# S5 outputs: the copies of the scan states dealt anew to GpSimd, ScalarE and VectorE, and the gated unit's first weights asked for ahead of y

## The chip, the cores and the metric

One core of a Trainium2 chip runs the whole program. The metric is the device time in microseconds (us), smaller is better. The engines are TensorE (PE in the profile, its weight loads PEld), VectorE (DVE), ScalarE (ACT), GpSimd (POOL) and SyncE (SP), whose queue issues most of the DMAs.

## The reference, cut to what matters

The program is a trunk of two layers over 512 latent and 256 context tokens of width 1024, all in fp32. Each layer is a half-step SwiGLU network, a token mixer and another half-step SwiGLU network. The mixer of layer 0 is a bidirectional S5 state space model, that of layer 1 gated linear attention (GLA). The change lies at the end of the S5 mixer:

```
y = scan forward(u) + flip(scan backward(flip u)) + d_skip * u      # states times C, both directions
z = gelu(y) @ w_glu + b_glu                                         # 1024 -> 2048
val, gate = split(z, 2);   x = x + gate_mod * (val * sigmoid(gate)) # the gated unit
```

## The kernel before

Products of fp32 matrices are made from three products of parts: `mm3` (L113 to L115) multiplies a weight's high half `whi` with the high and the low part of the activation, and its low half `wlo` with the high part. `whi` is cast by ScalarE (L88), `wlo` is a subtraction on VectorE (L89). Both follow the weight's DMA into `wraw`, which SyncE issues; `wraw` has four buffers, `whi` and `wlo` five each.

The scan runs on VectorE and leaves its states in a tile `r` (`big` in the profile). `outputs` makes the result in eight tiles, kt = 0 to 7. For each, `states` copies the states into `xs[kt % 2]`, one of two buffers: per half of the groups (g) and real or imaginary part (a) the forward states (z = 0) in one copy of 64 x 380, the backward states (z = 1) in two, 64 x 124 and 64 x 256. A table of two by two functions, indexed [z][a], names the engine of each copy. For tiles 0 and 1 the first 80 steps are copied early by ScalarE, beside the scan. Then TensorE makes 16 sums of two products (L912), VectorE adds the skip term half by half (L914), ScalarE applies the gelu (L916), and SyncE stores y to DRAM. While tiles 1 to 3 run, the y stored before is read back (`yk`, three buffers); the other five are read back in `glu`.

`glu` first casts each yk into the parts of `h` (two casts on ScalarE, two subtractions on VectorE per k; L937 and L938). `h` lies in the memory of the scan states, so that the first cast waits until all copies of tile 7 are done. Then, for each j, it asks for two weights (q = 0 the value, q = 1 the gate) and `step` multiplies.

The order on each engine is not that of the code: a scheduler simulates the program's timeline when it is built and puts each engine's instructions, and each queue's DMAs, in the order of its plan, for the whole program.

Of the kernel before, what the change touches and what calls it, by code (L numbers as in the profile page):

```python
# [15 lines left out]
P = 128  # L16
D = 1024
# [10 lines left out]
def fview(t, off, dims, p0=0, n=P):  # L28

    b = t[p0:p0 + n]  # L30
    return bass.AP(b.tensor, b.offset + off, [list(b.ap[0])] + [list(d) for d in dims])


def dview(ap, off, dims):

    return bass.AP(ap.tensor, ap.offset + off, [list(d) for d in dims])
# [286 lines left out]
def kinds(s, e):  # L323

    return [(i, max(s, a), min(e, z)) for i, (a, z) in enumerate(((0, CTX), (CTX, TOK))) if max(s, a) < min(e, z)]
# [146 lines left out]
N5 = TOK // L5  # L472
# [4 lines left out]
class S5:  # L477
# [323 lines left out]
    def states(self, kt, kind, evac):  # L801


        c, nc, r = self.c, self.c.nc, self.r
        n0, n = ((0, NX5), (NX5, N5 - NX5))[kind]
        m = (32, 64)[kind]
        u = self.u[kt][:, :, n0:n0 + n]
        banks = [c.bank() for _ in range(kind + 1)]
        for part in range(2):
            for z in range(2):  # L810
                i = (part * 2 + z) * 4 * n
                b, o = banks[i // 512], i % 512
                for q in range(4):
                    for g in range(2):
                        for p0 in range(64 * g, 64 * g + 64, m):
                            nc.tensor.matmul(b[p0:p0 + m, o + q * n:o + (q + 1) * n],
                                             self.rm[2 * kt + part][:, z * 512 + q * P + p0:z * 512 + q * P + p0 + m],
                                             u[:, 2 * q + g], start=True, stop=True)
                src = fview(b, o + z * (n - 1), [(n, 4), (1 - 2 * z, n)])
                dst = fview(r, n0 * P + part * 64 + z * 32 + 4 * kt, [(1, 4), (P, n)])  # L820
                last = (nc.scalar.copy if evac[part] else nc.vector.tensor_copy)(out=dst, in_=src)
        return last
# [38 lines left out]
    def outputs(self, pool, ahead, yp, last):  # L861


        c, nc, r = self.c, self.c.nc, self.r
        loaded, self.ys = {}, []

        def load(kt):
            om = [c.spare() for _ in range(2)]
            for z in range(2):
                c.dma(om[z], self.O[kt][z])  # L870
            return om
        for kt in range(ahead):
            loaded[kt] = load(kt)
        xs = [pool.tile([P, 2, 8, N5], F32, name=f"xs{i}", tag=f"xs{i}", bufs=1) for i in range(2)]
        for x in xs:
            nc.gpsimd.memset(x[:, 0, :, 0:1], 0.0)
        def states(kt, s0, s1, copies):

            x = xs[kt % 2]
            nc.gpsimd.memset(x[:, 1, :, NX5 - 1:NX5], 0.0)  # L880
            for g in range(2):
                for a in range(2):
                    def move(z, lo, hi, to, step):

                        lo, hi = max(lo, s0), min(hi, s1)
                        if lo >= hi:
                            return
                        at, to = (lo, to(lo)) if step > 0 else (hi - 1, to(hi - 1))
                        src = fview(r, at * P + a * 64 + z * 32 + 4 * kt, [(1, 4), (step * P, hi - lo)], 64 * g, 64)
                        dst = fview(x, z * 8 * N5 + g * N5 + to, [(2 * N5, 4), (1, hi - lo)], 64 * a, 64)  # L890
                        copies[z][a](out=dst, in_=src)
                    move(0, 0, N5 - 1, lambda s: s + 1, 1)
                    move(1, 0, NX5 - 1, lambda s: NX5 - 2 - s, -1)
                    move(1, NX5 - 1, N5 - 1, lambda s: NX5 + N5 - 2 - s, -1)
        early = 80
        with c.tc.issue_after(last.ins):
            for kt in range(2):
                states(kt, 0, early, [[nc.scalar.copy] * 2] * 2)

        def work():  # L900
            for kt in range(KT):
                x = xs[kt % 2]
                om = loaded.pop(kt) if kt in loaded else load(kt)
                states(kt, early if kt < 2 else 0, N5, [[nc.scalar.copy, nc.gpsimd.tensor_copy], [nc.vector.tensor_copy] * 2])
                y = pool.tile([P, 8, N5], F32, tag="y5", name="y5", bufs=4)
                for h in range(2):
                    b = c.bank()
                    for i in range(4):
                        g = 4 * h + i
                        o = b[:, i * N5:(i + 1) * N5]  # L910
                        for z in range(2):
                            nc.tensor.matmul(o, om[z][:, g * P:(g + 1) * P], x[:, z, g], start=(z == 0), stop=(z == 1))  # L912
                    yh = y[:, 4 * h:4 * h + 4].rearrange("p g n -> p (g n)")
                    nc.vector.tensor_tensor(out=yh, in0=b[:, :4 * N5], op=ALU.add,  # L914
                                            in1=self.u[kt][:, 4 * h:4 * h + 4].rearrange("p g n -> p (g n)"))
                nc.scalar.activation(y, y, AF.Gelu_apprx_tanh)  # L916
                c.dma(dview(self.Y, kt * P * TOK, [(N5, P), (C5 * TOK, 8), (1, N5)]), y)
                if 0 < kt < 4:
                    self.load_y(yp, kt - 1)
        return work  # L920

    def glu(self, pool, parts, last, after):


        c, nc, m = self.c, self.c.nc, self.m
        wg = self.ins["s5_w_glu"][0].rearrange("(k p) e -> p k e", p=P)
        yh, yl = c.h[:, 0], c.h[:, 1]
        for k in range(KT):
            if k >= len(self.ys):
                self.load_y(pool, k)  # L930
            y = self.ys[k]
            for lo, hi, view in ((0, CTX, lambda t: t.rearrange("p (n i) -> p i n", i=L5)),
                                 (CTX, TOK, lambda t: t.rearrange("p (w i r) -> p i r w", i=L5, r=8))):
                h, l, src = view(yh[:, k, lo:hi]), view(yl[:, k, lo:hi]), y[:, :, lo // L5:hi // L5]
                if lo:
                    src = src.rearrange("p i (r w) -> p i r w", r=8)
                nc.scalar.copy(out=h, in_=src)  # L937
                nc.vector.tensor_tensor(out=l, in0=src, in1=h.bitcast(F32), op=ALU.subtract)  # L938

        def step(j, w, s, e):  # L940
            n = e - s
            banks = [c.bank() for _ in range(2)]
            order = [(k, q) for k in range(KT) for q in range(2)] if j == 0 else \
                    [(k, q) for q in range(2) for k in range(KT)]
            for i, (k, q) in enumerate(order):
                c.mm3(banks[q][:, :n], w[q], slice(k * P, (k + 1) * P), (yh[:, k, s:e], yl[:, k, s:e]),
                      k == 0, k == KT - 1)
                if i % 4 == 3:
                    c.tick()
            sg = c.tmp.tile([P, 512], F32, tag="sg", name="sg", bufs=2)[:, :n]  # L950
            nc.scalar.activation(sg, banks[1][:, :n], AF.Sigmoid, bias=m.col("s5_b_glu", KT + j))
            nc.vector.scalar_tensor_tensor(out=sg, in0=banks[0][:, :n], scalar=m.col("s5_b_glu", j), in1=sg,
                                           op0=ALU.add, op1=ALU.mult)
            for i, a, z in kinds(s, e):
                nc.vector.scalar_tensor_tensor(out=c.xT[:, j, a:z], in0=sg[:, a - s:z - s],
                                               scalar=m.mod[0][:, i, 5, j:j + 1], in1=c.xT[:, j, a:z],
                                               op0=ALU.mult, op1=ALU.add)
        ws = []
        for j in range(KT):
            ws.append([c.weight(wg[:, :, q * D + j * P:q * D + (j + 1) * P]) for q in range(2)])  # L960
            if j < KT - 3:
                for s, e in parts:
                    step(j, ws[j], s, e)
        for s, e in last:
            for j in range(KT - 3, KT):
                step(j, ws[j], s, e)
            after(s, e)
# [645 lines left out]
```

## Time and profile before

| | |
|---|---|
| median of three runs | 2886.12 us (2885.47 to 2887.6) |
| the profiled execution | 2881.74 us, its span 2880.0 us |
| granted TensorE clock, mean | 0.968 of full speed |
| TensorE busy | 2733.7 us, 95% of the span |
| VectorE, ScalarE, GpSimd busy | 1795.0 us (62%), 855.2 us (30%), 22.2 us (1%) |
| the scan's end on VectorE, the outputs' start on TensorE | 801.4 us |
| end of the last output tile on TensorE | 839.7 us |

Times within the program are us from the start of the span. Busy time is the time in which an engine executes; the wait ahead of an instruction is put down to the work that released it last. The profiled execution is a run of its own, so its time lies beside the median and not in it.

### The profile page before, as it was taken

To read this page: it belongs to the slowest core of one execution; us is meant where nothing else is said; L and a number is where in the kernel's file an instruction comes from. 1 tells how busy PE (TensorE), PEld (TensorE's weight loads), DVE (VectorE), ACT (ScalarE), POOL (GpSimd) and SP (SyncE) were. 2 spreads that over 40 slices of the span, in tenths; PEclk is the share of its full clock that TensorE was granted. 3 is DMA by queue.
4 is the path that set the end of the run, shared out by engine and by line. 5 is a ranking of instruction groups with operands and counts; after the bars stand their busy time and mean duration, and the time that the engine had idled before them with its cause. 6 is when DMAs were issued, how large, how long until landed. Compare 5 with 4: busy or idle time off the path is not lost. (4 is left out here: it accounts for less than half of the span.)

```text
span 2880.0 us, 44946 instructions
## 1 busy us (share of the span) xinstructions
PE 2733.7 (95%) x18231; PEld 2577.7 (90%) x18231; DVE 1795.0 (62%) x4080; ACT 855.2 (30%) x1386; POOL 22.2 (1%) x57
## 2 busy tenths in 40 slices
PE   7999999997479999999999999999999899799998
PEld 5899999996269999999999999999998788788887
DVE  6698999436993565556526555665368786643433
ACT  4222222225362422111124221121245453332223
POOL 0000000000010000000000000000000000000000
PEclk9999999997689999999999999999999899899999
DMA  6535554516662133333311342333103112233320
GB/s 226 169 113 158 150 157 137 175 62 193 227 180 81 48 103 109 99 101 116 96 59 38 110 125 88 110 104 95 54 16 89 45 52 67 66 117 95 92 91 30
DMA packets 396045, 305.43 MB, mean 106 GB/s; under 512 B 57995, under 2 KB 344189, under 8 KB 395837
## 3 DMA queue, kind: packets, MB, share of 16 engines
q1 hardware_dynamic: 391228, 293.12, 34.0%
q10 hardware_dynamic: 4608, 9.44, 0.9%
q8 instruction: 143, 2.34, 0.3%
q14 instruction: 66, 0.53, 0.1%
HBM read 275.77 MB, written 30.41 MB: 106 GB/s over the span
## 5 line engine op out<-in xcount | busy, mean ns | idle before, releaser
L115 PE MATMUL bank<-h,wlo 128*128 128x384 f32 (+3 forms) x3160 | 1048.3, 332 | 5.0 <-DVE wlo L89 5.0
L114 PE MATMUL bank<-h,whi 128*128 128x384 f32 (+3 forms) x3160 | 1049.8, 333 | 0.3 <-DVE h L219 0.3
L113 PE MATMUL bank<-h,whi 128*128 128x384 f32 (+3 forms) x3160 | 1044.6, 333 | 2.2 <-ACT h L218 2.2
L88 ACT CAST whi<-wraw 128x1024 fp32r<-128x1024 f32 x313 | 327.5, 1048 | 993.4 <-PE bank L114 934.3
L115 PEld LDWEIGHTS bank<-h,wlo 128*128 128x128 f32 (+1 forms) x3160 | 594.6, 188 | 22.9 <-DVE wlo L89 5.3
L113 PEld LDWEIGHTS bank<-h,whi 128*128 128x128 f32 (+1 forms) x3160 | 593.3, 189 | 22.9 <-ACT h L218 2.7
L114 PEld LDWEIGHTS bank<-h,whi 128*128 128x128 f32 (+1 forms) x3160 | 596.3, 189 | 18.0 <-DVE h L219 0.8
L89 DVE TENSOR_TENSOR wlo<-wraw,whi 128x1024 fp32r<-128x1024 f32 x313 | 381.2, 1219 | 253.0 <-ACT whi L88 245.3
L114 PE MATMUL bank<-ml,whi 128*128 128x384 f32 (+2 forms) x1360 | 447.7, 330 | 0.0
L113 PE MATMUL bank<-mh,whi 128*128 128x384 f32 (+2 forms) x1360 | 446.5, 331 | 0.6 <-DVE xT L279 0.6
L115 PE MATMUL bank<-mh,wlo 128*128 128x384 f32 (+2 forms) x1360 | 446.0, 329 | 0.0
L279 DVE SCALAR_TENSOR_TENSOR xT<-bank,hg,xT 128x256 f32<-128x256 f32 (+2 forms) x488 | 220.7, 499 | 200.2 <-PE bank L115 199.8
L264 DVE TENSOR_TENSOR sg<-sg,bank 128x384 f32<-128x384 f32 (+2 forms) x166 | 89.5, 539 | 355.9 <-PE bank L115 342.7
L113 PEld LDWEIGHTS bank<-mh,whi 128*128 128x128 f32 x1360 | 256.7, 189 | 7.9 <-DVE xT L279 1.0
L114 PEld LDWEIGHTS bank<-ml,whi 128*128 128x128 f32 x1360 | 257.1, 189 | 6.6 <-issue 0.4
L115 PEld LDWEIGHTS bank<-mh,wlo 128*128 128x128 f32 x1360 | 256.2, 188 | 6.5 <-issue 0.2
L427 DVE SCALAR_TENSOR_TENSOR adaacc<-wraw,cs,adaacc 128x512 f32<-128x512 f32 x336 | 236.6, 744 | 14.8 <-DMA wraw<-in_ada_w_dram 14.5
L265 ACT CAST mh<-sg 128x384 fp32r<-128x384 f32 (+2 forms) x166 | 83.4, 502 | 305.9 <-DVE sg L264 304.8
L263 ACT ACTIVATE sg<-bank 128x384 f32<-128x384 f32 (+2 forms) x166 | 79.5, 479 | 199.8 <-PE bank L115 199.8
L266 DVE TENSOR_TENSOR ml<-sg,mh 128x384 fp32r<-128x384 f32 (+2 forms) x166 | 89.8, 541 | 23.5 <-ACT mh L265 23.4
L150 ACT ACTIVATE sq<-xT 128x256 f32<-128x256 f32 (+1 forms) x126 | 52.4, 427 | 59.9 <-DVE xT L279 41.5
L201 DVE SCALAR_TENSOR_TENSOR nt<-xT,sc,bank 128x256 f32<-128x256 f32 (+2 forms) x136 | 61.9, 476 | 12.5 <-PE bank L182 9.3
(298 smaller groups left out, 2332.8 us busy)
## 6 DMA issues: line engine op xcount, KB each, us to landing
wraw<-in_ffn_w_in_dram SPq DMA_DIRECT2D x176, 512.0 KB, 3.8
wraw<-in_ada_w_dram SPq DMA_DIRECT2D x111, 512.0 KB, 3.8
wraw<-in_ffn_w_out_dram SPq DMA_DIRECT2D x88, 512.0 KB, 3.4
wraw<-in_gla_w_in_dram SPq DMA_DIRECT2D x24, 512.0 KB, 3.9
s5R<-s5r ACTq DMA_DIRECT2D x16, 512.0 KB, 3.1
s5O<-s5g SPq DMA_DIRECT2D x64, 128.0 KB, 2.9
wraw<-in_s_w_glu_dram SPq DMA_DIRECT2D x16, 512.0 KB, 4.8
big<-in_ada_w_dram SPq DMA_DIRECT2D x12, 512.0 KB, 8.5
```

The source lines that it names most:

```text
L88: nc.scalar.copy(out=hi[:, :n], in_=raw[:, :n])
L89: nc.vector.tensor_tensor(out=lo[:, :n], in0=raw[:, :n], in1=hi[:, :n].bitcast(F32), op=ALU.subtract)
L113: mm(out, wh, a[0], start=first, stop=False)
L114: mm(out, wh, a[1], start=False, stop=False)
L115: mm(out, wl, a[0], start=False, stop=last)
L201: nc.vector.scalar_tensor_tensor(out=t[:, a - s:z - s], in0=self.xT[:, k, a:z], scalar=sc[i][:, k:k + 1], in1=r[:, a - s:z - s], op0=ALU.m ...
L263: nc.scalar.activation(sg, banks[0][:, :e - s], AF.Silu)
L264: nc.vector.tensor_mul(sg, sg, banks[1][:, :e - s])
L265: nc.scalar.copy(out=mh[:, o], in_=sg)
L266: nc.vector.tensor_tensor(out=ml[:, o], in0=sg, in1=mh[:, o].bitcast(F32), op=ALU.subtract)
L279: nc.vector.scalar_tensor_tensor(out=self.xT[:, d, a:z], in0=banks[d][:, a - s:z - s], scalar=gate[i][:, d:d + 1], in1=self.xT[:, d, a:z], ...
L427: nc.vector.scalar_tensor_tensor(out=acc[:, v], in0=w[:, k], scalar=col, in1=acc[:, v], op0=ALU.mult, op1=ALU.add)
```

## The change

In the table of `outputs` both forward copies go to GpSimd (one was ScalarE's), and of the backward copies those with a = 0 go to ScalarE and those with a = 1 stay on VectorE. The copies of the first 80 steps stay with ScalarE. In `glu`, the call that asks for the weights of j = 0 moves ahead of the loop over y; those of the other j stay where they were. Four lines are added, so that later lines have numbers higher by four (L937 becomes L941, L1243 becomes L1247).

```diff
--- before.py
+++ after.py
@@ -901,7 +901,7 @@
             for kt in range(KT):
                 x = xs[kt % 2]
                 om = loaded.pop(kt) if kt in loaded else load(kt)
-                states(kt, early if kt < 2 else 0, N5, [[nc.scalar.copy, nc.gpsimd.tensor_copy], [nc.vector.tensor_copy] * 2])
+                states(kt, early if kt < 2 else 0, N5, [[nc.gpsimd.tensor_copy] * 2, [nc.scalar.copy, nc.vector.tensor_copy]])
                 y = pool.tile([P, 8, N5], F32, tag="y5", name="y5", bufs=4)
                 for h in range(2):
                     b = c.bank()
@@ -925,6 +925,10 @@
         c, nc, m = self.c, self.c.nc, self.m
         wg = self.ins["s5_w_glu"][0].rearrange("(k p) e -> p k e", p=P)
         yh, yl = c.h[:, 0], c.h[:, 1]
+
+        def weights(j):
+            return [c.weight(wg[:, :, q * D + j * P:q * D + (j + 1) * P]) for q in range(2)]
+        ws = [weights(0)]
         for k in range(KT):
             if k >= len(self.ys):
                 self.load_y(pool, k)
@@ -955,9 +959,9 @@
                 nc.vector.scalar_tensor_tensor(out=c.xT[:, j, a:z], in0=sg[:, a - s:z - s],
                                                scalar=m.mod[0][:, i, 5, j:j + 1], in1=c.xT[:, j, a:z],
                                                op0=ALU.mult, op1=ALU.add)
-        ws = []
         for j in range(KT):
-            ws.append([c.weight(wg[:, :, q * D + j * P:q * D + (j + 1) * P]) for q in range(2)])
+            if j:
+                ws.append(weights(j))
             if j < KT - 3:
                 for s, e in parts:
                     step(j, ws[j], s, e)
```

The names y_8752, y_8784, y_8822, y_8864, y_8906, y_8946, y_8986 and y_9026 below are y of tiles 0 to 7, xs_8663 and xs_8664 the two buffers of the copied states.

SyncE's queue from the store of the first y on; s5Y is y in DRAM, s5O the S5 output matrices. Before:

```order
L70 DMA s5Y<-y_8752 128x8x96
L70 DMA wraw<-s5O_789 128x1024
L70 DMA s5Y<-y_8784 128x8x96
L70 DMA yk<-s5Y 128x768
L70 DMA wraw<-s5O_790 128x1024
L70 DMA s5Y<-y_8822 128x8x96
L70 DMA yk<-s5Y 128x768
L70 DMA wraw<-in_s_w_glu_dram 128x8x128
L70 DMA s5Y<-y_8864 128x8x96
L70 DMA wraw<-in_s_w_glu_dram 128x8x128
L70 DMA yk<-s5Y 128x768
L70 DMA s5Y<-y_8906 128x8x96
```

After the change:

```order
L70 DMA s5Y<-y_8752 128x8x96
L70 DMA wraw<-s5O_789 128x1024
L70 DMA yk<-s5Y 128x768
L70 DMA s5Y<-y_8784 128x8x96
L70 DMA wraw<-s5O_790 128x1024
L70 DMA yk<-s5Y 128x768
L70 DMA s5Y<-y_8822 128x8x96
L70 DMA yk<-s5Y 128x768
L70 DMA wraw<-in_s_w_glu_dram 128x8x128
L70 DMA s5Y<-y_8864 128x8x96
L70 DMA wraw<-in_s_w_glu_dram 128x8x128
L70 DMA s5Y<-y_8906 128x8x96
```

Each of the first three read-backs (yk) stands ahead of the next store of y, and the first weights (in_s_w_glu), which stood behind the second of them, stand behind the third; five more read-backs come later, four of them in a row behind the store of y_8986.

ScalarE around the gelu of tile 4, with the cast of the first weights. Before:

```order
L916 ACTIVATE y_8864<-y_8864 128x768
L891 COPY xs_8663<-big 64x4x95 x2
L916 ACTIVATE y_8906<-y_8906 128x768
L88 CAST whi<-wraw 128x1024
L891 COPY xs_8664<-big 64x4x95 x2
L916 ACTIVATE y_8946<-y_8946 128x768
```

After the change:

```order
L916 ACTIVATE y_8864<-y_8864 128x768
L88 CAST whi<-wraw 128x1024
L891 COPY xs_8663<-big 64x4x31
L891 COPY xs_8663<-big 64x4x64
L891 COPY xs_8663<-big 64x4x31
L891 COPY xs_8663<-big 64x4x64
L916 ACTIVATE y_8906<-y_8906 128x768
```

The cast of the first weights stands ahead of the copies of tile 6 (xs_8663) and of the gelu of tile 4, where it stood behind that gelu; the copies are now the backward shapes.

ScalarE at the end of the outputs, around the gelu of the last tile. Before:

```order
L916 ACTIVATE y_8946<-y_8946 128x768
L937 CAST h<-yk 128x8x32
L937 CAST h<-yk 128x64x8
L937 CAST h<-yk 128x8x32
L937 CAST h<-yk 128x64x8
L937 CAST h<-yk 128x8x32
L937 CAST h<-yk 128x64x8
L916 ACTIVATE y_8986<-y_8986 128x768
L916 ACTIVATE y_9026<-y_9026 128x768
L88 CAST whi<-wraw 128x1024 x2
```

After the change:

```order
L941 CAST h<-yk 128x64x8
L941 CAST h<-yk 128x8x32
L941 CAST h<-yk 128x64x8
L941 CAST h<-yk 128x8x32
L941 CAST h<-yk 128x64x8
L941 CAST h<-yk 128x8x32
L941 CAST h<-yk 128x64x8
L916 ACTIVATE y_9026<-y_9026 128x768
L88 CAST whi<-wraw 128x1024 x2
```

Ahead of the gelu of y_9026 stand now twelve casts of y, all behind the gelu of y_8986; it was six, ahead of that gelu. Behind it follow two casts of weights as before.

VectorE at the same place, the adds of the last tile. Before:

```order
L938 TENSOR_TENSOR h<-yk,h 128x8x32
L938 TENSOR_TENSOR h<-yk,h 128x64x8
L914 TENSOR_TENSOR y_8986<-bank,u 128x384
L938 TENSOR_TENSOR h<-yk,h 128x8x32
L938 TENSOR_TENSOR h<-yk,h 128x64x8
L938 TENSOR_TENSOR h<-yk,h 128x8x32
L938 TENSOR_TENSOR h<-yk,h 128x64x8
L914 TENSOR_TENSOR y_9026<-bank,u 128x384 x2
L89 TENSOR_TENSOR wlo<-wraw,whi 128x1024 x3
```

After the change:

```order
L942 TENSOR_TENSOR h<-yk,h 128x64x8
L942 TENSOR_TENSOR h<-yk,h 128x8x32
L942 TENSOR_TENSOR h<-yk,h 128x64x8
L914 TENSOR_TENSOR y_9026<-bank,u 128x384
L942 TENSOR_TENSOR h<-yk,h 128x8x32
L942 TENSOR_TENSOR h<-yk,h 128x64x8
L942 TENSOR_TENSOR h<-yk,h 128x8x32
L942 TENSOR_TENSOR h<-yk,h 128x64x8
L914 TENSOR_TENSOR y_9026<-bank,u 128x384
L942 TENSOR_TENSOR h<-yk,h 128x8x32
L942 TENSOR_TENSOR h<-yk,h 128x64x8
L89 TENSOR_TENSOR wlo<-wraw,whi 128x1024 x3
```

The first low halves of weights (L89) stood behind the low parts of three yk and stand now behind those of six; between the two adds of the last tile lie four of these subtractions.

TensorE in the GLA stage (layer 1), one of its heads; `gqc` and `gkc` are scaled queries and keys, lines 1110 to 1112 project values. Before:

```order
L1110 MATMUL bank<-whi,h 128x256
L1111 MATMUL bank<-wlo,h 128x256
L1112 MATMUL bank<-whi,h 128x256
L1243 MATMUL aux<-gqc,gkc 128x128 x24
L182 MATMUL bank<-ident,rs 128x128 x4
L1110 MATMUL bank<-whi,h 128x256
L1111 MATMUL bank<-wlo,h 128x256
L1112 MATMUL bank<-whi,h 128x256
```

After the change:

```order
L1114 MATMUL bank<-whi,h 128x256
L1115 MATMUL bank<-wlo,h 128x256
L1116 MATMUL bank<-whi,h 128x256
L1247 MATMUL aux<-gqc,gkc 128x128 x28
L1292 MATMUL aux<-ident,gkf 128x128 x4
L182 MATMUL bank<-ident,rs 128x128 x4
L1114 MATMUL bank<-whi,h 128x256
L1115 MATMUL bank<-wlo,h 128x256
L1116 MATMUL bank<-whi,h 128x256
```

The row of products of gqc and gkc has 28 instead of 24, and four transposes (L1292) have moved up behind it.

## Rows read from the trace of the kernel before

**Rows 1.** The page, part 1: busy time, share of the span and instructions of each engine.

```profile
PE 2733.7 (95%) x18231; PEld 2577.7 (90%) x18231; DVE 1795.0 (62%) x4080; ACT 855.2 (30%) x1386; POOL 22.2 (1%) x57
```

**Rows 2.** The waits of TensorE between 800 and 900 us: engine, tile and line that waited, what it waited for; total us, times, longest.

```profile
PE bank L912 <- POOL xs L891: 41.1, 1, 41.1
PE bank L912 <- DVE xs L891: 5.9, 5, 1.2
PE bank L115 <- DVE wlo L89: 5.0, 1, 5.0
```

**Rows 3.** Stretches of the S5 outputs and of the gated unit's start: stretch and its length in us, then busy us and instructions of PE, PEld, DVE, ACT and POOL, the granted TensorE clock, the DMA share and GB/s.

```profile
805.90:839.70 33.80, 27.86 (x238) 26.88 (x238) 31.32 (x64) 20.17 (x25) 13.07 (x18) 1.00 0.60 174
839.80:843.30 3.50, 0.30 (x2) 0.04 (x1) 3.50 (x6) 2.10 (x4) 0.00 (x0) 1.00 0.76 240
843.40:845.10 1.70, 0.00 (x0) 0.00 (x0) 1.67 (x3) 1.13 (x2) 0.00 (x0) 0.50 0.93 216
845.20:850.10 4.90, 4.90 (x16) 4.90 (x17) 4.32 (x5) 4.90 (x7) 0.00 (x0) 0.50 1.05 310
850.30:900.00 49.70, 49.70 (x285) 49.70 (x285) 25.96 (x35) 21.29 (x28) 0.00 (x0) 1.00 0.57 153
```

**Rows 4.** Timeline of TensorE from 836 to 846 us: start, us, engine, line, operation, out<-in, count, and in brackets the idle time before it and its releaser. L912 is the last tile's products, L113 to L115 those of the gated unit.

```profile
836.79 0.46 PE L912 MATMUL bank<-xs,wraw 128*128 128x96 f32 x2
...
839.49 0.42 PE L113 MATMUL bank<-h,whi 128*128 128x384 f32 x1
...
845.12 0.69 PE L115 MATMUL bank<-h,wlo 128*128 128x384 f32 x1 [5.02 <-DVE wlo L89]
```

**Rows 5.** Timeline of ScalarE from 828 to 853 us (L88 casts a weight's high half, L937 casts y).

```profile
831.16 1.03 ACT L88 CAST whi<-wraw 128x1024 fp32r<-128x1024 f32 x1
...
836.90 4.36 ACT L937 CAST h<-yk 128x256 fp32r<-128x256 f32 x6 [0.68 <-DVE xs L891]
...
850.99 1.70 ACT L937 CAST h<-yk 128x256 fp32r<-128x256 f32 x2 [0.36 <-DMA yk<-s5Y]
```

**Rows 6.** Timeline of VectorE from 834 to 846 us (L938 is the low part of y, L914 the add of a tile, L89 a weight's low half).

```profile
838.53 1.08 DVE L938 TENSOR_TENSOR h<-yk,h 128x512 fp32r<-128x512 f32 x1 [0.30 <-ACT h L937]
...
839.97 3.04 DVE L938 TENSOR_TENSOR h<-yk,h 128x256 fp32r<-128x256 f32 x4
842.91 1.02 DVE L914 TENSOR_TENSOR y<-bank,u 128x384 f32<-128x384 f32 x2
843.85 1.22 DVE L89 TENSOR_TENSOR wlo<-wraw,whi 128x1024 fp32r<-128x1024 f32 x1
```

**Rows 7.** Timeline of VectorE over the state copies of one tile.

```profile
815.35 2.57 DVE L891 COPY xs<-big 64x124 f32<-64x124 f32 x4
...
818.42 1.33 DVE L891 COPY xs<-big 64x124 f32<-64x124 f32 x4
```

**Rows 8.** Instructions by line, operation and shape between 800 and 863 us: line engine op out<-in, count | busy us, mean ns of one | idle time before them and its releasers.

```profile
L891 ACT COPY xs<-big 64x380 f32<-64x380 f32 x12 | 10.6, 880 | 5.4 <-PE bank L912 5.3
...
L914 DVE TENSOR_TENSOR y<-bank,u 128x384 f32<-128x384 f32 x16 | 8.8, 557 | 2.7 <-PE bank L912 2.3
L88 ACT CAST whi<-wraw 128x1024 fp32r<-128x1024 f32 x8 | 8.3, 1052 | 2.3 <-DMA wraw<-in_s_w_glu_dram 2.2
L916 ACT ACTIVATE y<-y 128x768 f32<-128x768 f32 x8 | 6.7, 842 | 13.3 <-DVE y L914 13.3
```

**Rows 9.** The same view of ScalarE between 739 and 800 us, where it makes the early copies.

```profile
L891 ACT COPY xs<-big 64x320 f32<-64x320 f32 x8 | 5.9, 739 | 27.7 <-DVE big L504 27.6
L891 ACT COPY xs<-big 64x196 f32<-64x196 f32 x8 | 4.2, 524 | 0.1
L891 ACT COPY xs<-big 64x124 f32<-64x124 f32 x8 | 3.2, 402 | 0.1
```

**Rows 10.** Timeline of GpSimd: its first two late copies together, then those of one tile one by one (the same tile as in rows 7).

```profile
807.26 2.34 POOL L891 COPY xs<-big 64x380 f32<-64x380 f32 x2 [4.76 <-PE bank L912]
...
815.33 0.85 POOL L891 COPY xs<-big 64x380 f32<-64x380 f32 x1 [2.74 <-PE bank L912]
...
816.24 1.20 POOL L891 COPY xs<-big 64x380 f32<-64x380 f32 x1
817.50 0.12 POOL L880 MEMSET xs<- 128x8 f32 x1
```

**Rows 11.** Timeline of SyncE's queue (SPq): the issues of the first store of y, of the gated unit's first weights, and of the sixth yk.

```profile
811.71 0.37 SPq L70 DMA_DIRECT2D s5Y<-y  x1
...
822.34 0.79 SPq L70 DMA_DIRECT2D wraw<-in_s_w_glu_dram  x1
...
845.25 1.93 SPq L70 DMA_DIRECT2D yk<-s5Y  x1
```

**Rows 12.** DMA issues between 805 and 870 us: out<-in, queue, count, KB each, median us from issue to landing.

```profile
wraw<-in_s_w_glu_dram SPq DMA_DIRECT2D x12, 512.0 KB, 4.8
s5Y<-y SPq DMA_DIRECT2D x8, 384.0 KB, 3.4
```

**Rows 13.** The waits of TensorE in the GLA stage, 2100 to 2500 us.

```profile
PE aux L1243 <- DVE gqc L1240: 6.8, 5, 2.3
PE bank L182 <- DVE rs L175: 2.9, 2, 2.3
```

## The prediction

> **What bounds the kernel now.** I read the engine totals first: TensorE is busy 2733.7 of 2880.0 us [rows 1], so a change in the S5 stage is worth what it takes from TensorE's few gaps there and nothing else. Next the waits of TensorE from 800 to 900 us [rows 2]. The last wait for the scan (41.1 us) ends before the changed copies begin. Behind it there are only two: 5.9 us in five pieces for VectorE's copies, and one piece of 5.0 us for the low half of the first gated-unit weights. The stretches [rows 3] place them: while the eight output tiles run (805.9 to 839.7), TensorE works 27.86 of 33.80 us and VectorE 31.32, so VectorE sets that pace. From 839.8 to 845.1 TensorE is all but idle, and what its restart waits for is on VectorE and ScalarE. So the number that decides is **the time at which TensorE restarts in the gated unit**, 845.12 us [rows 4]: from there it works without a gap, at half clock to 850.1 (granted 0.50), then at full clock [rows 3]. Whatever the tiles gain counts only if the restart comes earlier.
>
> Why 845.12? The chain, in order of time: casts of the stored y begin at 836.90 [rows 5], after the last state copy; their second halves (the subtraction that gives the low part) follow on VectorE, with the adds of the last two tiles among them, the last pair of adds at 842.91; only then comes the first weight's low half, 843.85 to 845.07 [rows 6]. The weight's high half was cast long before, at 831.16 [rows 5].
>
> **What the change does to the copies.** Per tile VectorE now makes eight backward copies, four beside GpSimd's (2.57 us) and four alone (1.33 us) [rows 7], and two adds of 0.56 us [rows 8]: 5.02 us a tile, the pace seen. After: VectorE keeps four copies and the adds, at most 2.57 + 1.12 = 3.7 us. ScalarE gets backward copies: two times a 64x124 (0.402 us) and a 64x256; the latter shape is not in its rows, between 64x196 at 0.524 and 64x320 at 0.739 it interpolates to 0.63 [rows 9]. So 2.06 us a tile, with the gelu 0.84 [rows 8] 2.9 us. GpSimd gets four forward copies instead of two. Beside VectorE a copy took 0.85 and the next 1.20, the memset 0.12 [rows 10]; gaps of 0.06: T = 2 x (0.85 + 1.20) + 0.24 + 0.12 = 4.5 us a tile. GpSimd becomes the slowest copier, and still beats 5.02.
>
> Two bounds of T. From below, 4 x 0.85 + 0.36 = 3.8 (no disturbance). From above: if a VectorE copy and a GpSimd copy never run at once, T = 4 x 0.85 + 1.33 + 0.36 = 5.1. The row speaks for some exclusion: VectorE's four copies took 1.24 us longer beside GpSimd [rows 7]. I take 4.5, since the 1.20 already contains a wait. GpSimd's first changed tile begins near its present 807.26 [rows 10]; say 806.9. Five periods and a last tile of 3.8 (VectorE done) give its last copy at 806.9 + 22.5 + 3.8 = 833.2, by the upper bound 836.2.
>
> [...]
>
> **What the order does to the loads.** The diff alone doesn't say this; the order does. On SyncE's queue each read-back of y (yk) now stands ahead of the next store of y, and it must wait until the store before it has landed. y0 is issued at 811.71 [rows 11] (the gelu before it stands behind a like amount of ScalarE copies, 2.06 us against two of 0.88 [rows 8]); 3.4 us to land [rows 12]: yk0 at 815.1; 0.53 for its issue, y1 at 815.7, landed 819.1; then y2 at 819.7, landed 823.1; yk2, then the first weights at 823.7, against 822.34 now [rows 11]. They land 4.8 us later [rows 12]: **828.5**. So "asked for ahead of y" ends with the weights asked for 1.4 us later.
>
> ScalarE now casts them ahead of the copies of tile 6, not behind part of them, so its queue stands until 828.5. Then: cast 1.05 [rows 8] to 829.6; copies of tile 6 to 831.6; gelu 4 to 832.4; copies of tile 7 to 834.5; gelu 5 and 6 to 836.1. Behind the waiting cast stand thus all of tiles 6 and 7. TensorE's last tile runs from 834.5 (now 836.79 [rows 4]), done about 2.3 us earlier. The casts of y start at **836.1** (now 836.90): GpSimd's 833.2 lies under it, and its upper bound just about meets it. Of the gain of half a microsecond per tile some 0.8 us is left here.
>
> **What the order does behind it.** Now gelu 7 follows six casts (k0 to k2); in the changed order it follows twelve (k0 to k5), and VectorE's last add stands behind ten second halves. yk3, yk4 and yk5 need the buffers of k0 to k2 freed. k0 is free 2.7 us after the casts begin (836.90 to 838.53 + 1.08 [rows 5, 6]): 838.8. A yk load took at least the 3.4 us of a store of the same size [rows 12], and up to 5.7 (issue 845.25, cast at 850.99, which waited for it [rows 11, 5]); I take 4.5: 843.3. Three pairs of casts at 4.36/3 = 1.45 us [rows 5] end at 847.6, the second halves of k4 at 847.3, the add (0.56) at 847.9, gelu 7 at 848.7. Behind it stands the cast of the second weights (1.05): 849.8. TensorE, whose order after the first two products is now the second weight's products, restarts at **849.9** instead of 845.12. The first low half is done by 850.8 (two second halves of k5 from 847.9, 1.6 us, then 1.22 [rows 6]), before the six products at half clock ahead of it are through (16 took 4.90 us [rows 3], so 1.8 us). After that nothing is late: k0 to k5 lie ready.
>
> With the clock I reckon nothing: TensorE is at half clock from 843.4 until about 5 us after its restart [rows 3, 4]; with a longer idle time the same half-clock stretch follows a later restart.
>
> Cost: 849.9 − 845.12 = **+4.8 us**. Bounds: yk loads at 3.4 us, then yk5 (asked for when k2 is free, 842.0) lands at 845.4, gelu 7 begins at 846.9, restart 848.9: +3.7; loads at 5.7: +6.0.
>
> **The rest of the program.** The same instructions stand in another order in the GLA stage, since the scheduler plans on. TensorE waits there 6.8 us in five pieces for gqc and 2.9 us for rs [rows 13]. Now 24 products of L1243 stand in one row, afterwards 28, and the next head's are spread. No row prices an order; I take 0, with plus or minus 6.8 as bounds.
>
> **Sum.** The profiled execution took 2881.74 us, below the median 2886.12 of the three runs shown; 2881.74 + 4.8 = 2886.5, and against the median 2886.12 + 4.8 = 2890.9, said as **2891**. 0.2% is 5.8 us, about what a measurement of this kernel can tell from no change.
>
> **The rivals.**
> *Loads earlier, restart later by less.* If y1 and y2 land faster than 3.4 us (a 3.0 would bring 2 x 0.4), and the casts start with GpSimd's 833.2, then all of the tail comes 2.9 us earlier: restart 847.0, +1.9, 2888. Against it: the weights' 4.8 us is a median under just such traffic. 0.12.
> *GLA order gains (the faster side).* If the row of 28 hides the 6.8 us of gqc, the sum is 4.8 − 6.8 = −2.0, 2884; with the 2.9 of rs too, −4.9. For it: a longer row gives gqc more time. Against: the spread in the next head gives it less. It turns the sign when more than 4.8 of the 9.7 us go. 0.12, of which 0.04 beyond 0.2%.
> *GpSimd's period decides (slower).* From T = 5.1 on GpSimd's last copy, not ScalarE, starts the casts. At 5.6 (the exclusive 5.1 and half a microsecond of handing over, as the 1.20 against 0.85 shows 0.35 for one) it ends at 806.9 + 28 + 4 = 838.9, casts 2.8 later, restart 852.7, +7.6: 2893.7. For it: VectorE's 1.24. Against: 1.20 was the worst neighbour seen. 0.13.
> *GLA order costs.* If the five gqc waits double, 4.8 + 6.8 = 11.6: 2897.7; half of it 2894. 0.13.
> *Forecast*, +3.7 to +6.0 (2889.8 to 2892.1): 0.50, of which 0.07 lies over 5.8 us.
>
> **Numbers.** Slower by over 0.2%: 0.07 + 0.13 + 0.12 = 0.32. Faster by over 0.2%: 0.05. Within: 0.63. The range leaves out the better half of the GLA gain below 2885 and the worse part of the GLA cost above 2896, together under 0.2; its ends come from these two rivals.
>
> **What would show it.** Right: yk0 on SyncE's queue at about 815 with y1 behind it; the first weights' cast on ScalarE waiting for its DMA until 828 to 829; GpSimd's four copies at 4.4 to 4.6 us a tile; casts of y from 836; gelu 7 at 848; TensorE idle for 10 us or more, ended by ScalarE's cast of the second weights, not by VectorE's low half. Wrong: casts starting from a wait for GpSimd; a restart before 848; GLA waits that differ by more than 3 us.

## The result and the profile after

The changed kernel takes 2897.6 us (median of seven runs, 2892.51 to 2899.95) against 2887.6 us of the kernel before beside it; the ratio is 1.0033 with a 95% interval of 1.0023 to 1.0043. It is slower by about 9.5 us (0.33% of 2887.6), twice the forecast of 4.8, and its median lies beyond the range's end of 2896.

The profiled execution spans 2894.2 us (before 2880.0). It can be cut at three places: TensorE's first product of S5 tiles behind the scan, its restart in the gated unit, and the last update of `xT` by the gated unit. The part ahead of the first place is the same work and varies by itself: it ended at 801.44 in the trace of before and at 804.31 in a second trace of the same program. So all lengths below count from the first product. Before: 43.7 us to the restart, 185.5 to the gated unit's end, 1893.0 from there to the program's end. After: 53.6, 194.8 and 1895.5. In these two traces the change thus costs 9.3 us up to the gated unit's end and 2.5 behind it, 11.8 together; the timed runs say 9.5, with an interval of 6.6 to 12.4.

The waits of TensorE from 800 to 900 us in the changed kernel (as rows 2 of before):

```profile
PE bank L912 <- POOL xs L891: 41.5, 1, 41.5
PE bank L113 <- ACT whi L88: 9.7, 1, 9.7
PE bank L912 <- issue: 5.8, 1, 5.8
PE bank L912 <- POOL xs L880: 1.6, 3, 0.6
```

The five waits for VectorE's copies and the 5.0 us for the low half [rows 2] are gone. In their place stand 9.7 us for ScalarE's cast of the second weights, ahead of the gated unit, and 5.8 us inside the outputs, for which the profile names no releaser. What TensorE did there, and its restart (timeline, as rows 4):

```profile
803.84 0.74 PE L912 MATMUL bank<-xs,whi 128*128 128x96 f32 x2 [41.47 <-POOL xs L891]
...
836.87 0.71 PE L912 MATMUL bank<-xs,whi 128*128 128x96 f32 x2 [5.78 <-issue]
...
857.45 0.69 PE L113 MATMUL bank<-h,whi 128*128 128x384 f32 x1 [9.69 <-ACT whi L88]
```

The products of tile 6 stop until 836.87. ScalarE's timeline says why (as rows 5; L941 is the cast of y):

```profile
823.63 0.84 ACT L916 ACTIVATE y<-y 128x768 f32<-128x768 f32 x1
834.91 1.04 ACT L88 CAST whi<-wraw 128x1024 fp32r<-128x1024 f32 x1 [10.43 <-DMA wraw<-in_s_w_glu_dram]
835.86 1.86 ACT L891 COPY xs<-big 64x124 f32<-64x124 f32 x4
...
843.83 0.84 ACT L916 ACTIVATE y<-y 128x768 f32<-128x768 f32 x1 [2.61 <-DVE y L914]
844.58 4.32 ACT L941 CAST h<-yk 128x256 fp32r<-128x256 f32 x6
850.23 1.56 ACT L941 CAST h<-yk 128x256 fp32r<-128x256 f32 x2 [1.33 <-DMA yk<-s5Y]
...
855.63 0.84 ACT L916 ACTIVATE y<-y 128x768 f32<-128x768 f32 x1
856.37 1.97 ACT L88 CAST whi<-wraw 128x1024 fp32r<-128x1024 f32 x2
```

From 824.47 on ScalarE stands before the cast of the first weights, 10.43 us, and the copies of tile 6 come only behind it, at 835.86: TensorE's "issue" is this wait. Then come the casts of y, 844.58, and the last gelu, which now follows all twelve of those in the order shown ahead. SyncE's queue shows why the weights came so late (as rows 11):

```profile
814.80 0.37 SPq L70 DMA_DIRECT2D s5Y<-y  x1
...
819.17 0.32 SPq L70 DMA_DIRECT2D yk<-s5Y  x1
819.59 0.39 SPq L70 DMA_DIRECT2D s5Y<-y  x1
...
823.92 0.32 SPq L70 DMA_DIRECT2D yk<-s5Y  x1
824.33 0.39 SPq L70 DMA_DIRECT2D s5Y<-y  x1
829.37 0.32 SPq L70 DMA_DIRECT2D yk<-s5Y  x1
829.74 0.47 SPq L70 DMA_DIRECT2D wraw<-in_s_w_glu_dram  x1
...
847.29 5.93 SPq L70 DMA_DIRECT2D yk<-s5Y  x4
```

Three times a read-back (yk) waits for the store ahead of it, 4.4, 4.3 and 5.0 us from the store's issue to the read-back's, and each time the next store, and at the end the first weights, stand behind it. GpSimd's timeline (as rows 10):

```profile
818.63 3.97 POOL L891 COPY xs<-big 64x380 f32<-64x380 f32 x4
...
822.97 3.95 POOL L891 COPY xs<-big 64x380 f32<-64x380 f32 x4
...
831.60 3.72 POOL L891 COPY xs<-big 64x380 f32<-64x380 f32 x4
```

Its period is 4.34 us (818.63 to 822.97), and its last copy ends at 835.3, nine us ahead of the first cast of y. TensorE waits for it 1.6 us in three pieces, by the waits above (L880 is GpSimd's memset behind the copies of a tile); the casts of y don't wait for it.

### The profile page after: what moved, and what is told of

Its sections match the earlier page's. It is cut to its first block, busy times and chain, and to the rows that moved or that the text cites. A ratio compares the mean times of both kernels' runs of the same rounds, so it can differ in the third digit from the quotient of the medians.

```text
span 2894.2 us, 44954 instructions
## 1 busy us (share of the span) xinstructions
PE 2738.7 (95%) x18231; PEld 2583.3 (89%) x18231; DVE 1786.2 (62%) x4052; ACT 857.8 (30%) x1398; POOL 34.2 (1%) x73
## 5 line engine op out<-in xcount | busy, mean ns | idle before, releaser
L113 PE MATMUL bank<-h,whi 128*128 128x384 f32 (+3 forms) x3160 | 1046.2, 334 | 12.4 <-ACT whi L88 9.7
L115 PE MATMUL bank<-h,wlo 128*128 128x384 f32 (+3 forms) x3160 | 1047.2, 332 | 0.0
L88 ACT CAST whi<-wraw 128x1024 fp32r<-128x1024 f32 x313 | 327.6, 1048 | 997.1 <-PE bank L114 934.1
L113 PEld LDWEIGHTS bank<-h,whi 128*128 128x128 f32 (+1 forms) x3160 | 593.0, 189 | 33.1 <-ACT whi L88 9.9
L115 PEld LDWEIGHTS bank<-h,wlo 128*128 128x128 f32 (+1 forms) x3160 | 594.9, 188 | 17.6 <-issue 0.6
L89 DVE TENSOR_TENSOR wlo<-wraw,whi 128x1024 fp32r<-128x1024 f32 x313 | 381.2, 1220 | 247.9 <-ACT whi L88 244.7
L113 PE MATMUL bank<-mh,whi 128*128 128x384 f32 (+2 forms) x1360 | 446.1, 331 | 1.2 <-DVE xT L279 1.2
L115 PE MATMUL bank<-mh,wlo 128*128 128x384 f32 (+2 forms) x1360 | 446.0, 329 | 0.0
L113 PEld LDWEIGHTS bank<-mh,whi 128*128 128x128 f32 x1360 | 256.4, 189 | 8.4 <-DVE xT L279 1.5
L115 PEld LDWEIGHTS bank<-mh,wlo 128*128 128x128 f32 x1360 | 256.2, 188 | 6.5 <-issue 0.2
```

What stands on the lines that cost most here:

```text
L88: nc.scalar.copy(out=hi[:, :n], in_=raw[:, :n])
L89: nc.vector.tensor_tensor(out=lo[:, :n], in0=raw[:, :n], in1=hi[:, :n].bitcast(F32), op=ALU.subtract)
L113: mm(out, wh, a[0], start=first, stop=False)
L115: mm(out, wl, a[0], start=False, stop=last)
```

## The experiments

Three things were in question: the order on SyncE's queue, the order at the end (twelve casts ahead of the last gelu), and the copies themselves on GpSimd. A fourth is the order of the rest of the program. Each diff below is cut to the lines that matter; that of copies_alone is against the kernel before, all others against the changed kernel, and the lines an experiment adds shift its line numbers (the cast of y is L941 to L958). The helper `issue_after(x)` makes the scheduler place what its block makes behind x on x's engine or queue, with no wait added. The lengths, from the profiled executions, in us:

| kernel | first product to restart | to the gated unit's end | from there to the end | ratio to before (95%) |
|---|---|---|---|---|
| before | 43.7 | 185.5 | 1893.0 | 1 |
| changed | 53.6 | 194.8 | 1895.5 | 1.0033 (1.0023 to 1.0043) |
| copies_alone | 53.2 | 194.4 | 1895.6 | 1.0043 (1.0031 to 1.0055) |
| stores_first | 45.8 | 186.7 | 1893.2 | 1.0004 (0.9996 to 1.0013) |
| gelu_first | 47.0 | 188.4 | 1893.3 | 1.0013 (1.0004 to 1.0021) |
| both_undone | 39.6 | 181.3 | 1893.7 | 0.9980 (0.9972 to 0.9989) |
| cast_behind | 47.4 | 189.1 | 1895.2 | 1.0019 (1.0010 to 1.0028) |
| parts_first | no restart | 178.5 | 1896.4 | 0.9985 (0.9976 to 0.9993) |

The last two lengths, added and set against before, give +11.8, +11.5, +1.3, +3.1, −3.5, +5.7 and −3.7 us from the changed kernel down; each lies within its ratio's interval.

**copies_alone** and **weights_alone** split the change in two.

```diff
-                states(..., [[nc.scalar.copy, nc.gpsimd.tensor_copy], [nc.vector.tensor_copy] * 2])
+                states(..., [[nc.gpsimd.tensor_copy] * 2, [nc.scalar.copy, nc.vector.tensor_copy]])
```

> The new table of copies alone, the weights asked for where they were. Its built program has the same order on every engine and queue as the changed kernel, and the weights' move alone gives the order of the kernel before. Queue theory, tail theory and a theory of GpSimd's pace all expect the changed kernel's time again: ratio 1.0033 within 0.001, stage from TensorE's first S5 product to its restart in the gated unit 53 to 54.5 us (before 43.7, after 53.6). If the move of the weights had a price of its own, it would come out nearer to 1.000.

The table of copies alone took 2897.14 us, ratio 1.0043, and ScalarE stood 10.37 us before the first weights' cast. weights_alone is the changed kernel with the old table. The weights' move alone is in the built program no move at all: the scheduler puts every instruction where it stood.

> The weights' move alone; its built program has the order of the kernel before on every engine and queue. Stage from TensorE's first S5 product to its restart 43.5 to 44 us, and from the end of the gated unit to the program's end 1893.0 us again (before 1893.0) if that rest belongs to the order and not to the single execution; 1 us or more away if it varies by itself.

In its one execution it took 44.3 us to the restart, 186.4 to the gated unit's end, and 1891.7 behind; the last misses the expected 1893.0 by 1.3. So the whole loss comes with the table of copies, and "asked for ahead of y" changed nothing, in either direction.

**stores_first** holds each of the first three read-backs behind the next store.

```diff
-                c.dma(dview(self.Y, ...), y)
+                st = c.dma(dview(self.Y, ...), y)
                 if 0 < kt < 4:
-                    self.load_y(yp, kt - 1)
+                    with c.tc.issue_after(st.ins):
+                        self.load_y(yp, kt - 1)
```

> The changed kernel, but each of the first three read-backs is held behind the next store on SyncE's queue. Queue theory: the weights land at about 827 to 829 instead of 834.9 (counted in the changed kernel's trace), ScalarE's wait for them falls from 10.4 to 3 to 4 us, TensorE's idle 5.8 us inside the outputs and the half clock behind it go too, so the stage falls from 53.6 to 45 to 47 us and the time to 2 to 4 us over before. Tail theory (the twelve casts ahead of the last gelu are what costs): the stage stays at 52 or more. GLA-order theory: the time stays within 1 us of the changed kernel whatever the stage does.

ScalarE's timeline and TensorE's restart in it:

```profile
830.41 1.05 ACT L88 CAST whi<-wraw 128x1024 fp32r<-128x1024 f32 x1 [5.03 <-DMA wraw<-in_s_w_glu_dram]
...
837.60 4.32 ACT L942 CAST h<-yk 128x256 fp32r<-128x256 f32 x6
...
851.26 0.69 PE L113 MATMUL bank<-h,whi 128*128 128x384 f32 x1 [10.49 <-ACT whi L88]
```

The wait for the weights is 5.03 instead of 10.43 us (3 to 4 were expected; asked for at 822.83, they took 7.6 us to land, in the changed kernel 5.2), the 5.8 us of TensorE inside the outputs are gone, and the stage falls by 7.8 us, from 53.6 to 45.8. The tail from the first cast to the restart stays: 837.60 to 851.26 is 13.7 us (12.9 in the changed kernel). 1.0004 is the time of the kernel before again, where 2 to 4 us over it were expected; the interval ends at 3.8.

**gelu_first** leaves the queue and holds the casts and subtractions from k = 3 on behind the last gelu and the last add.

```diff
+                    self.add = nc.vector.tensor_tensor(out=yh, ...)
+                self.tail = nc.scalar.activation(y, y, AF.Gelu_apprx_tanh)
...
+                    if k > 2:
+                        behind.enter_context(c.tc.issue_after(self.tail.ins))
+                        behind.enter_context(c.tc.issue_after(self.add.ins))
```

> The changed kernel, but the casts and subtractions of y from k = 3 on are held behind the last gelu and the last add; the queue is as in the changed kernel. Tail theory: from the first cast of y to TensorE's restart 8.5 to 9.5 us instead of 12.9, stage 49 to 50 us, time 5 to 6 us over before. Queue theory alone: the wait of 10.4 us for the weights stays, and the restart gains no more than 2 us. Both hold if the 10.4 stays and the tail shrinks by 3.5 to 4.5.

```profile
830.87 1.04 ACT L88 CAST whi<-wraw 128x1024 fp32r<-128x1024 f32 x1 [9.78 <-DMA wraw<-in_s_w_glu_dram]
...
840.55 4.31 ACT L945 CAST h<-yk 128x256 fp32r<-128x256 f32 x6
847.16 0.84 ACT L916 ACTIVATE y<-y 128x768 f32<-128x768 f32 x1 [2.30 <-DVE y L914]
...
848.31 0.69 PE L115 MATMUL bank<-h,wlo 128*128 128x384 f32 x1 [4.59 <-DVE wlo L89]
```

The wait for the weights stays, 9.78 us; from the first cast to the restart it is now 7.8 us (840.55 to 848.31) instead of 12.9, and TensorE waits for VectorE's low half again, as before. The stage is 47.0, somewhat better than the 49 to 50 expected. Of the 6.6 us gained 5.1 lie behind the first cast of y; the other 1.5 lie ahead of it, in work that the hold doesn't touch.

**both_undone** has both holds.

> Both holds together, the copies as changed. If the two orders are the whole loss, the stage is 41 to 43 us (before 43.7) and the time 0 to 3 us under before. If GpSimd's copies themselves cost (its pace, or VectorE held off by it), the stage stays at 45 or more with the casts of y released by GpSimd. GLA-order theory: the time stays 2 us or more over before although the stage is as short as before.

```profile
825.74 1.04 ACT L88 CAST whi<-wraw 128x1024 fp32r<-128x1024 f32 x1 [4.55 <-DMA wraw<-in_s_w_glu_dram]
...
833.05 4.33 ACT L946 CAST h<-yk 128x256 fp32r<-128x256 f32 x6
839.66 0.84 ACT L916 ACTIVATE y<-y 128x768 f32<-128x768 f32 x1 [2.29 <-DVE y L914]
...
840.81 0.69 PE L115 MATMUL bank<-h,wlo 128*128 128x384 f32 x1 [4.60 <-DVE wlo L89]
```

39.6 us to the restart (41 to 43 were expected), 4.1 less than before and 14.1 less than changed; the two holds apart gave 7.8 and 6.6. The median is 2880.71 us, the ratio 0.998, and it beats both kernels, by more than the 0 to 3 us under before that were expected. So with these two orders held the new table of copies is worth some 4 us (the casts of y begin 31.8 us behind the first product, before 35.5), and the two orders cost 14. Not every order is as it was: ScalarE still stands 4.55 us before the weights' cast. GpSimd's pace is out as a cause of the loss. It is close to being the next limit: its last copy ends at 832.2, 0.9 us ahead of the first cast of y, and TensorE waits for its buffers 2.3 us in five pieces.

**cast_behind** asks through what the late weights cost. The queue is that of the changed kernel, but the first weights' cast is held behind ScalarE's copies of the last tile (`moved`, the last copy that ScalarE got).

```diff
-        ws = [weights(0)]
+        with c.tc.issue_after(self.moved.ins):
+            ws = [weights(0)]
```

> The changed kernel with its queue order, but the cast of the first weights is held behind ScalarE's copies of the last tile. If the late weights cost because the copies of tiles 6 and 7 stand behind their cast, the copies now run at once, TensorE has no 5.8 us idle time inside the outputs, the casts of y begin some 30 to 31 us after TensorE's first S5 product (changed kernel: 40.7) and the stage is 44 to 47 us (changed: 53.6, stores first: 45.8), although the weights land as late as before. If what costs is the late landing itself, or the late third store behind the read-backs, the stage stays at 51 or more.

```profile
838.98 1.04 ACT L88 CAST whi<-wraw 128x1024 fp32r<-128x1024 f32 x1 [2.81 <-DMA wraw<-in_s_w_glu_dram]
839.93 1.57 ACT L918 ACTIVATE y<-y 128x768 f32<-128x768 f32 x2
841.41 4.29 ACT L944 CAST h<-yk 128x256 fp32r<-128x256 f32 x6
```

The weights come as late as in the changed kernel (cast 30.9 us after the first product at 808.11; there 31.1), but ScalarE waits 2.81 us instead of 10.43, and the stage is 47.4, 6.2 less. So most of the price of the late weights was what stood behind their cast on ScalarE. The casts of y began at 33.3 us, not at 30 to 31, and the stage ends just above the expected 44 to 47: gelus 5 and 6 still stand behind the held cast. A second trace [its expectation below] gave 46.3 us, 1.1 less, where 0.5 were allowed for. Single traces of one program scatter that much in this stage (stores_first 45.8 and 46.4, before 43.7 and 44.3), far less than the 6.2 to 14.1 us read here.

**parts_first** adds to both_undone that the first two weights are asked for in the last output tile and that their two halves are made ahead of the casts of y. The last gelu is held behind the second high half.

```diff
+                if kt == KT - 1:
+                    with c.tc.issue_after(self.moved.ins):
+                        self.first = [c.weight(wg[:, :, q * D:q * D + P]) for q in range(2)]
...
+                    if k < 3:
+                        behind.enter_context(c.tc.issue_after(c.hi.ins))
+                        behind.enter_context(c.tc.issue_after(c.lo.ins))
```

> Both orders undone as before, and besides the first two weights are asked for in the last output tile, with their two high halves cast right behind ScalarE's last copies and their low halves made ahead of the casts of y. If TensorE's last idle time of 4.6 us (both undone) is only the order, TensorE goes from the last tile into the gated unit with less than 3 us idle, the clock stays at full speed or falls for a shorter time, and the time is 4 to 8 us below both undone (ratio to before 0.995 to 0.997). If the read-backs of y set the pace behind it, the gain is under 2 us, and the waits appear at the casts of k = 3 or later.

```profile
841.37 0.39 PE L918 MATMUL bank<-xs,wraw 128*128 128x96 f32 x2
841.54 0.42 PE L113 MATMUL bank<-h,whi 128*128 128x384 f32 x1
841.79 0.34 PE L114 MATMUL bank<-h,whi 128*128 128x384 f32 x1
841.97 0.33 PE L115 MATMUL bank<-h,wlo 128*128 128x384 f32 x1
...
PE bank L918 <- POOL xs L880: 2.0, 1, 2.0
PE bank L114 <- DVE h L959: 0.9, 3, 0.4
PE bank L113 <- ACT h L958: 0.4, 1, 0.4
```

TensorE goes from the last tile (L918 here) into the gated unit without a gap, at 0.17 to 0.18 us a product, and its waits up to 900 us there are 0.9 and 0.4 us. Up to the gated unit's end that is 2.9 us better than both_undone (178.5 against 181.3). But the rest of the program is 2.7 us longer (1896.4 against 1893.7), and the time is no better: 0.9985 against 0.998. The expected 4 to 8 us did not come.

Some of them went in the outputs: ahead of the last tile TensorE waits 2.0 us for GpSimd, whose last four copies took 5.63 us (in both_undone 3.86). VectorE made the two low halves beside them:

```profile
828.20 3.97 POOL L891 COPY xs<-big 64x380 f32<-64x380 f32 x4
...
832.54 5.63 POOL L891 COPY xs<-big 64x380 f32<-64x380 f32 x4
...
834.28 1.39 DVE L89 TENSOR_TENSOR wlo<-wraw,whi 128x1024 fp32r<-128x1024 f32 x1 [0.40 <-ACT whi L88]
...
836.05 1.41 DVE L89 TENSOR_TENSOR wlo<-wraw,whi 128x1024 fp32r<-128x1024 f32 x1
```

The second trace shows 5.64 us and the same 2.1 us of waiting. That the subtractions hold the copies up is read from this coincidence; no run tests it by itself.

Whether such a rest belongs to the order or to the single execution was asked with second traces.

> A second trace of the kernel with the stores first. If the rest behind the gated unit belongs to the order, it is 1893.2 us again within 0.5; if it is the single execution's, it may as well be 1895.5 as in the changed kernel, whose waits in the GLA stage are the same.

> A second trace of the kernel with the cast held behind the copies. Order theory: rest 1895.2 us within 0.5. Single-execution theory: it differs by 1 or more. Stage 47.4 within 0.5 either way.

> A second trace of the kernel with the first parts ahead of the casts of y. Order theory: rest 1896.4 us within 0.5, so that the gain of 2.9 us up to the gated unit's end against both undone is given back behind it in every execution. Single-execution theory: nearer to 1893.5.

The rests were 1893.0 (first trace 1893.2), 1894.7 (1895.2) and 1896.4 (1896.4); changed and copies_alone, the same order, had 1895.5 and 1895.6; before and weights_alone 1893.0 and 1891.7. Four pairs of one order agree within 0.6 us. The fifth, before's, differs by 1.3, which its expectation had named as a sign that a rest varies by itself. Different orders lie up to 4.7 apart. So the rest goes with the order, with some scatter, and the changed kernel's is longer by 2.5 us against one trace of before and by 3.8 against the other.

The difference arises in the GLA stage. At the update of `xT` that comes 1123 us behind the gated unit's end in before, the changed kernel is 0.8 us ahead; at the one that comes at 1564 us it is 2.5 us behind, and stays there to the end. Which wait makes it was not settled: those of the changed kernel are like those of stores_first (7.9 and 7.8 us for gqc, 2.5 and 2.5 for the cast of h), whose rest is 2.4 us shorter. A large part of these 2.4 us is TensorE's clock. The same stretch, some 1310 us behind the gated unit's end, in the changed kernel and in stores_first (columns as in rows 3):

```profile
2308.00:2318.00 10.00, 10.00 (x63) 9.84 (x63) 6.60 (x16) 7.72 (x14) 0.30 (x1) 0.83 0.03 10
...
2302.00:2312.00 10.00, 10.00 (x74) 10.00 (x73) 6.67 (x17) 7.98 (x15) 0.13 (x1) 1.00 0.01 3
```

TensorE is never idle in either, but its granted clock is 0.83 in the one and 1.00 in the other, and between the same two updates of `xT` around it the same 430 products take 67.3 and 65.7 us. It is not the whole account: the second trace of stores_first has such a stretch too (0.66 from 2295 to 2305), and its rest is 1893.0.

## Why the prediction was wrong

The forecast gave 4.8 us more and put 0.63 on a change within 0.2%; it became 9.5 us and more than 0.2%. The sign of the sum, the waits on the queue and on ScalarE, and what releases TensorE's restart were right. One term, the queue, was too small, and two that were set to nothing, the clock and the rest of the program, were not nothing.

**The copies.** GpSimd's period: 4.5 us forecast, 4.34 measured. ScalarE's four copies: 2.06 forecast, 1.86 to 2.02 measured behind the first four (2.21). That GpSimd would not decide holds.

**The queue** failed in size. First store to the weights' issue: 811.7 to 823.7, 12.0 us, forecast; 814.80 to 829.74, 14.9 us, measured. The step that failed is "3.4 us to land", the median of the stores' row [rows 12]. The three landings that the queue waited for took 4.4, 4.3 and 5.0, together 3.5 us more than forecast; the issues between them took 0.6 less. A median over eight stores, most of which nobody waited for, was taken as the price of a wait; the row of yk loads gave up to 5.7, and this bound was used for the loads only.

**From the weights' landing to the first cast of y**: forecast 828.5 to 836.1, 7.6 us; measured 834.91 to 844.58, 9.7. The step that failed is "With the clock I reckon nothing". The wait on ScalarE left TensorE idle for 5.78 us inside the outputs, and its granted clock, 1.00 from 825 to 833, was 0.50 from 834 on; in stores_first, without this idle time, it was 1.00 from 831 to 838. That the idle time lowered it is read from these two traces. The products behind it (columns as in rows 3):

```profile
836.90:843.20 6.30, 6.30 (x29) 6.30 (x30) 0.56 (x1) 4.25 (x8) 0.00 (x0) 0.50 0.44 117
```

Tile 6 ran at half clock (0.50). Gelu 6 waited 2.61 us for VectorE's add of these products (ScalarE's row at 843.83), and the casts stand behind gelu 6. The forecast had the idle time of TensorE only ahead of the gated unit and did not ask what a stop inside the outputs does. The half-clock stretch that it did count on came behind the later restart too, but shorter: 3.6 us (granted 0.50 from 857.45 to 861.0), before 5.0 (845.12 to 850.1).

**The tail**: forecast 13.8 us from the first cast to the restart, measured 12.9, released by ScalarE's cast of the second weights as forecast. The price of the twelve casts was thus right in size (without the last six ahead of the gelu it is 7.8 us, in gelu_first), but in part by luck: the first of the three late yk took 2.9 us to the cast that waited for it (847.29 to 850.23) and not the 4.5 assumed for all three, nor the 3.4 taken as the least, while they came one behind the other, so that ScalarE stood 0.44 us more before each of the next two.

**The start**: the first store comes 11.0 us after the first product instead of 10.3 before; "behind a like amount of ScalarE copies" missed 0.7 us. Most of that is the single trace: ScalarE's copies wait there for TensorE, which stayed at half clock (granted 0.50) for 6.0 us from its first product (803.84 to 809.86) and in the trace of before for 4.4 us (801.44 to 805.82). In gelu_first, with the changed kernel's copies and queue, the first store comes at 10.0 us.

Together, against the forecast restart and counted from the first product: 0.7 (the start) + 2.9 (queue) + 0.4 (the weights' landing, 5.2 instead of 4.8) + 2.1 − 0.9 = 5.2 us; the restart moved by 9.9 instead of 4.8. **The rest of the program** was set to 0 with 6.8 either way, since no row priced an order; it cost 2.5, and the cause in the GLA stage stays open in part.

Of the rivals, GpSimd's period did not come, and the GLA order cost, by a good third of the 6.8 us that its rival doubled, though not by that rival's mechanism: the waits for gqc rose only from 6.8 to 7.9. The range ended at 2896 because each case was counted alone; the landings, the clock and the order of the rest came together.

SyncE's queue itself stands while a read-back waits (11.0 us in three pieces for the stores of y): the stores of y1 and y2 were issued 0.42 and 0.41 us behind the read-back that had waited ahead of them (819.59 and 824.33), although their gelus had ended at 817.5 and 820.3.

## What to carry to other kernels

Where a scheduler plans the whole program, a change of four engine names can move a load past a store on a queue and cost more than the copies gain: read the built order of queues first, and for each waiting instruction list what stands behind it on its queue or engine. Price a wait for a transfer by the transfers that somebody waited for, not by a median over all of them (here 4.3 to 5.0 us against 3.4), and follow each new idle time of TensorE into its clock (here 0.50 granted behind 5.78 us). When an order turns out to be the loss, hold the two or three instructions in place and keep the change: here that turned 9.5 us slower into 6 us faster.

## What the runs showed of the hardware

GpSimd's and VectorE's copies excluded each other less than the upper bound of the prediction assumed. In one period of 4.34 us stand four copies of GpSimd (3.95), its memset (0.25) and four copies of VectorE (1.27 and 0.84 for two each). With the fastest copies seen, 4 x 0.85 [rows 10] and 1.33 for VectorE's four [rows 7], strict exclusion would need 3.4 + 1.33 + 0.25 = 5.0. The measured 4.34 fits no full exclusion of the spans as the profile shows them; whether a part of each span excludes the other engine no run tells apart. VectorE's timeline in that tile:

```profile
821.58 1.27 DVE L891 COPY xs<-big 64x124 f32<-64x124 f32 x2 [0.56 <-PE bank L912]
822.89 0.56 DVE L914 TENSOR_TENSOR y<-bank,u 128x384 f32<-128x384 f32 x1
823.48 0.84 DVE L891 COPY xs<-big 64x124 f32<-64x124 f32 x2
```

The part ahead of the S5 outputs scatters by itself: one and the same program reached its first S5 product at 801.93 and at 808.11 us in two executions (cast_behind), another at 803.84 and 807.59 (changed and copies_alone). A loss in one stage is read from that stage's own start.
